# Two feed-forwards whose down projections change orientation: tokens x 512 columns, summed in SBUF and turned by TensorE

## The chip, the cores and the metric

The kernel runs on one core of a Trainium2 chip. The metric is the device time of one execution in microseconds, the median of several runs. One further execution was taken with the hardware profiler; its rows are what the prediction reads. A core has TensorE (PE, with its weight loads shown apart as PEld), VectorE (DVE), ScalarE (ACT), GpSimd (POOL) and SyncE (SP), which here issues the DMAs. Each engine works through its own queue in order, and PE writes only to PSUM, of which there are eight banks of 128 x 512 fp32 words.

## The reference, cut to what matters

A trunk of two layers on 256 tokens of width 2048, all in fp32. Each layer has a mixer and a convolutional feed-forward, with adaptive shift, scale and gate vectors computed from one conditioning vector `c`. This case is about the feed-forwards and the normalisation in front of them:

```python
def conv_ffn(h, w_up, conv_w, conv_b, w_down):
    u = causal_dwconv(h @ w_up, conv_w, conv_b)      # 2048 -> 2 x 5632, three taps over tokens
    a, b = jnp.split(u, 2, axis=-1)
    return (jax.nn.silu(a) * b) @ w_down             # 5632 -> 2048

def reference(...):
    ...
    for i in range(2):
        mod = (c_act @ ada_w[i] + ada_b[i])[:, None, :]
        sh1, sc1, g1, sh2, sc2, g2 = jnp.split(mod, 6, axis=-1)
        h = rms_norm(x, norm_g[i, 0]) * (1.0 + sc1) + sh1
        y = even_mixer(h, ...) if i % 2 == 0 else odd_mixer(h, ...)
        x = x + g1 * y
        h = rms_norm(x, norm_g[i, 1]) * (1.0 + sc2) + sh2
        x = x + g2 * conv_ffn(h, ffn_w_up[i], ffn_conv_w[i], ffn_conv_b[i], ffn_w_down[i])
    return x
```

## The kernel before

The residual `xT` stays in SBUF with channels on the partitions: 16 tiles (`kt`) of 128 channels x 256 tokens. The feed-forward's 5632 hidden channels are 44 blocks of 128, dealt into four quarters of 11 (`QK`); a quarter first computes 22 up blocks (`a` and `b` of each hidden block in turn), then goes down with the 11 gated blocks of that quarter as its k range.

**Numbers.** Most products are made from two fp32r parts. ACT copies a piece of a raw weight to `whi` (L133), and DVE, or POOL, subtracts to get the rest, `wlo` (L139). Activations have the same two parts: `h` (from `Modulated`, L529 to L537) and `g`, the gated product (L678 on ACT, L679 on DVE). A product is hi x hi, hi x lo and lo x hi: three matmuls. Where weights are given whole, as `raw`, one fp32 matmul does it (L360).

**Orientation.** `mm_t` has the weight block as the stationary operand and the 256 tokens as columns; the result is channels x tokens, as `xT` wants it. With `pair`, which the second feed-forward uses, both token parts of the activation are sent as one matmul of 512 columns and the third as 256 (L349 to L353), and two halves of the bank are added afterwards (L689, L690). Without it there are three of 256 (L356 to L358). `mm_n` has 128 tokens as the stationary operand and up to 512 weight columns moving (L367 to L369, for the odd mixer's projections); its result is tokens x channels.

**Order.** The order on each engine is written by the code, with some helpers. `W.take()` gives the next weight piece (at most 1024 columns a partition) and has the split of the piece two further on written first (`AHEAD`); three buffers each of raw, `whi` and `wlo` are there. Every `take()` also runs `advance()`, which writes one step of each open chain in `steps` and starts one from `waiting`; `hook()`, which runs one entry of `hooks`; and `tick()`, which writes an adaptive product `ada` (DVE, L269) when the credit reaches one; `rate["ada"]` is added per piece. `W.share` is the part of the `wlo` subtractions that go to POOL, a quarter in the first feed-forward and none in the second; while `W.hold` is set, none goes to POOL and no `ada` is written. A modulation value that is needed and not there yet is computed on the spot (`modulation`).

**The start of a feed-forward.** The first seven up blocks (`FIRST`; six blocks, `FIRST_U`, in the odd mixer's input projection) are run as `h.outer(n)`: for each `kt`, raw fp32 weights against `xT` scaled by the gain alone, 257 columns, n open banks. While this goes on, the token statistics are finished (at `kt == STATS`, L443), turned into a row on all partitions by two diagonals `SPREAD` steps later (L418, L419, `bc` L454), and the 16 normalised tiles of `h` are made. The early blocks are multiplied by `bc` afterwards into tiles `u` (L709 to L713).

**The end of a quarter.** After the quarter's up blocks one more up block of the next quarter is run; then come 16 down blocks, each summed over 11 k in one bank and added to `xT` times the gate (`add_into_x`, L553). At k = 10 `gated` writes out everything still open (`drain`) and lifts the hold. The last quarter has no further block to run.

## Time and profile before

| | |
|---|---|
| median of 3 runs | 2373.77 us (2373.11 to 2376.73) |
| the profiled execution | 2380.04 us, span from first to last instruction 2378.3 us |
| busy, share of the span | PE 96%, PEld 85%, DVE 75%, ACT 44%, POOL 16% |
| mean granted TensorE clock | 0.988 |
| DMA | 596.36 MB, mean 251 GB/s |

The stages of the profiled execution that matter here are: the even mixer up to 512.98 us; the first feed-forward from there to 1296.25; the odd mixer to 1590.06; the second feed-forward to the end. A window's row gives the length of a stretch, then for each engine its busy time and, in brackets, its instructions, then the granted clock (1.00 is 2.4 GHz), the mean busy share of the DMA engines and GB/s. In a row of a stretch in order of time stand start, duration, engine, line, operation, output <- inputs, shapes and count; the last bracket is idle time ahead of it and what ended that. A raw fp32 matmul shows as two instructions. Matmul durations overlap, so that the pace is read from the starts.

### The profile page before, as it was taken

The page shows a single profiled execution, that of the slowest core. Times are in us where ns is not written, and L with a number is a line of the kernel's source. Part 1 is how long each engine was busy: PE and PEld are TensorE (multiplying, and loading weights), DVE is VectorE, ACT ScalarE, POOL GpSimd, SP SyncE. Part 2 cuts the span into 40 slices and gives each one's busy share as a digit, 9 for nine tenths or more (in the row PEclk, how much of TensorE's full clock was granted, in tenths as well). Part 3 has the DMA queues.
Part 4 walks back from the last instruction along what each step waited for, and adds up shares of the span by engine and source line. Part 5 has one row for each costly group of instructions (what it writes and reads, how often), then busy time and mean ns, then how long its engine had stood idle before and what let it go on. Part 6 is the DMA issues. An engine that isn't in the chain of part 4 may idle for free. (4 is left out here: it accounts for less than half of the span.)

```text
span 2378.3 us, 36086 instructions
## 1 busy us (share of the span) xinstructions
PE 2288.6 (96%) x14056; PEld 2019.1 (85%) x14056; DVE 1786.0 (75%) x2827; ACT 1053.7 (44%) x1884; POOL 379.4 (16%) x238
## 2 busy tenths in 40 slices
PE   6898999999999999999999999999999999999999
PEld 3476677889999999999999777998788888888888
DVE  7758689747968878887986877667976766766765
ACT  2021254116444544544544556447544544554553
POOL 4233435101322222222222020000000000000000
PEclk9999999999999999999999999999999999999999
DMA  9968754776878878978887853556856546545545
GB/s 383 426 231 328 307 197 174 271 264 250 321 264 334 334 283 312 335 281 314 340 301 268 310 203 115 160 171 241 324 182 210 180 157 210 181 156 203 190 150 169
DMA packets 96365, 596.36 MB, mean 251 GB/s; under 512 B 11457, under 2 KB 14145, under 8 KB 44097
## 3 DMA queue, kind: packets, MB, share of 16 engines
q1 hardware_dynamic: 96194, 594.06, 68.4%
q8 instruction: 110, 1.80, 0.3%
q14 instruction: 61, 0.50, 0.1%
HBM read 591.92 MB, written 2.10 MB: 250 GB/s over the span
## 5 line engine op out<-in xcount | busy, mean ns | idle before, releaser
L133 ACT ACTIVATE whi<-raw 128x1024 fp32r<-128x1024 f32 (+2 forms) x659 | 626.8, 952 | 775.3 <-PE bank L357 352.3
L139 DVE TENSOR_TENSOR wlo<-raw,whi 128x1024 fp32r<-128x1024 f32 (+2 forms) x586 | 660.5, 1129 | 366.1 <-ACT whi L133 365.6
L269 DVE CUSTOM_DVE_ANT_0 ada<-ada,cB,adab 128x2048 f32<-128x2048 f32 x192 | 468.9, 2445 | 26.6 <-DMA ada<-adaw 26.0
L352 PE MATMUL bank<-h,whi 128*128 128x512 f32 x1215 | 432.6, 398 | 0.0
L358 PE MATMUL bank<-h,wlo 128*128 128x256 f32 x1328 | 377.3, 284 | 5.5 <-POOL wlo L139 4.9
L356 PE MATMUL bank<-h,whi 128*128 128x256 f32 x1328 | 377.1, 284 | 0.0
L357 PE MATMUL bank<-h,whi 128*128 128x256 f32 x1328 | 376.5, 284 | 0.0
L353 PE MATMUL bank<-h,wlo 128*128 128x256 f32 x1215 | 342.8, 282 | 5.5 <-DVE wlo L139 5.5
L139 POOL TENSOR_TENSOR wlo<-raw,whi 128x1024 fp32r<-128x1024 f32 (+2 forms) x73 | 192.1, 2634 | 667.4 <-ACT whi L133 601.3
L352 PEld LDWEIGHTS bank<-h,whi 128*128 128x128 f32 x1215 | 228.3, 188 | 51.3
L358 PEld LDWEIGHTS bank<-h,wlo 128*128 128x128 f32 x1328 | 255.6, 192 | 6.8 <-POOL wlo L139 5.7
L357 PEld LDWEIGHTS bank<-h,whi 128*128 128x128 f32 x1328 | 255.7, 193 | 0.0
L356 PEld LDWEIGHTS bank<-h,whi 128*128 128x128 f32 x1328 | 255.6, 192 | 0.0
L353 PEld LDWEIGHTS bank<-h,wlo 128*128 128x128 f32 x1215 | 229.4, 189 | 15.2 <-DVE wlo L139 12.0
L352 PE MATMUL bank<-g,whi 128*128 128x512 f32 x640 | 235.2, 407 | 0.9 <-DVE g L679 0.9
L357 PE MATMUL bank<-g,whi 128*128 128x256 f32 x704 | 199.6, 284 | 0.9 <-DVE g L679 0.9
L358 PE MATMUL bank<-g,wlo 128*128 128x256 f32 x704 | 200.1, 284 | 0.3
L356 PE MATMUL bank<-g,whi 128*128 128x256 f32 x704 | 199.3, 283 | 0.8 <-ACT g L678 0.8
L353 PE MATMUL bank<-g,wlo 128*128 128x256 f32 x640 | 182.7, 285 | 0.0
L360 PE MATMUL bank<-hw,raw 128*128 128x256 f32 x640 | 150.7, 390 | 14.1 <-DMA raw<-ev 9.5
L360 PEld LDWEIGHTS bank<-hw,raw 128*128 128x128 f32 x640 | 122.0, 195 | 43.4 <-issue 20.0
L352 PEld LDWEIGHTS bank<-g,whi 128*128 128x128 f32 x640 | 123.7, 193 | 28.7 <-ACT y L697 1.2
(281 smaller groups left out, 3696.9 us busy)
## 6 DMA issues: line engine op xcount, KB each, us to landing
ada<-adaw SPq DMA_DIRECT2D x192, 1024.0 KB, 6.1
raw<-wup SPq DMA_DIRECT2D x162, 1024.0 KB, 5.8
raw<-wdn SPq DMA_DIRECT2D x128, 704.0 KB, 4.2
raw<-out SPq DMA_DIRECT2D x44, 512.0 KB, 3.9
raw<-ev_a SPq DMA_DIRECT2D x16, 1024.0 KB, 4.9
raw<-ev SPq DMA_DIRECT2D x16, 896.0 KB, 14.7
raw<-wup SPq DMA_DIRECT2D x16, 896.0 KB, 4.7
raw<-cmp_w SPq DMA_DIRECT2D x8, 1024.0 KB, 8.5
```

Source lines behind the costliest of these rows:

```text
L133: nc.scalar.activation(hi[:, :n], raw, AF.Copy)
L139: eng.tensor_sub(lo[:, :n], raw, hi[:, :n].bitcast(F32))
L269: V.tensor_tensor_reduce(w, w, cB, 1.0, adab[:, i * 96 + j:i * 96 + j + 1], ALU.mult, ALU.add, m)
L352: PE.matmul(o, hi[:, s_], xx, start=start, stop=False)
L353: PE.matmul(o[:, :T], lo[:, s_], x[:, 0], start=False, stop=False)
L356: PE.matmul(o, hi[:, s_], x[:, 0], start=start, stop=False)
L357: PE.matmul(o, hi[:, s_], x[:, 1], start=False, stop=False)
L358: PE.matmul(o, lo[:, s_], x[:, 0], start=False, stop=stop)
L360: PE.matmul(o, w[:, s_], x, start=start, stop=stop)
```

## The change

In quarters 0 to 2 of both feed-forwards the down projection is done by `down_n`: `mm_n` with the gated block's tokens as the stationary operand and 512 weight columns moving, four chunks of 512 columns, two banks each. ACT copies the first quarter's banks into a tile `acc` (2 x 128 tokens x 2048, fp32, SBUF) and DVE adds those of the next two. During the last quarter's up blocks TensorE transposes `acc` by 128 x 128 blocks (`turn`), and DVE adds the result, times the gate, to `xT`; ten of sixteen `kt` are spread over the up blocks, the last six (`LATE`) stand between the up blocks and the last down projection, which keeps its form. The weights of the three quarters are laid out for this (loads of 4, 4 and 3 k of 512 columns). No up block is moved ahead of a down projection any more. In `gated` the open chains are written out only until the last gate's second part is, and during a hold every `take()` runs `advance()` twice. `FIRST` and `FIRST_U` become five, the statistics are asked for at `kt == 1`, the unsplit `h` moves from ACT to DVE, `u` lies in `acc`, and the rates of `ada` change.

```diff
-FIRST = 7
-FIRST_U = 6
+FIRST = 5
+FIRST_U = 5
+LATE = 6
-STATS = 3
+STATS = 1
-ADA_O = 0.7
+ADA_O = 0.3
-ADA_F0S = 0.4
+ADA_F0S = 0.3
-ADA_F1S = 0.5
+ADA_F1S = 0.1
+ADA_F1U = 0.08
+ADA_F1D = 0.05
...
         w = W.take()
         advance()
+        if W.hold:
+            advance()
         hook()
...
             f = sm.tile([P, T], F32, tag="hf", name="hf")
-            S.activation(f, t, AF.Identity, bias=sh, scale=gs)
+            V.tensor_scalar(f, t, gs, sh, op0=ALU.mult, op1=ALU.add)
...
             def gated(k, q):
                 if k == QK - 1:
-                    drain()
+                    while (q + 1) * QK - 1 not in gates:
+                        advance()
                     W.hold = False
+                    if late:
+                        steps.append(list(late))
+                        late.clear()
                 return gt[q, k // 2][:, k % 2]
+
+            def down_n(q):
+                for c in range(4):
+                    o = [bank() for _ in range(NT)]
+                    k = 0
+                    while k < QK:
+                        w, n = take()
+                        for u in range(n // 512):
+                            mm_n(o, w, slice(u * 512, (u + 1) * 512), gated(k, q), k == 0, k == QK - 1)
+                            k += 1
+                    def add(t, c=c, o=o):
+                        d = acc[:, t, c * 512:(c + 1) * 512]
+                        if q:
+                            V.tensor_tensor(d, d, o[t], op=ALU.add)
+                        else:
+                            S.activation(d, o[t], AF.Copy)
+                    waiting.append([lambda t=t, add=add: add(t) for t in range(NT)])
+
+            def turn(kt):
+                if kt % 2 == 0:
+                    turns[kt // 2] = bank()
+                p = turns[kt // 2][:, kt % 2 * T:(kt % 2 + 1) * T]
+                for t in range(NT):
+                    PE.transpose(p[:, t * P:(t + 1) * P], acc[:, t, kt * P:(kt + 1) * P], ident)
+                g = modulation(i, 80 + kt)
+                return lambda: V.scalar_tensor_tensor(xT[:, kt], p, g, xT[:, kt], op0=ALU.mult, op1=ALU.add)
...
-                for b in range(2 * QK * q + (q > 0) if q else FIRST, min(2 * QK * (q + 1) + 1, 2 * KF)):
+                end = q == NQ - 1
+                if end:
+                    hooks.extend([None] * 6)
+                    for kt in range(KD - LATE):
+                        hooks.append(lambda kt=kt: defer(turn(kt)))
+                        hooks.append(None)
+                for b in range(2 * QK * q if q else FIRST, 2 * QK * (q + 1)):
...
-                    follow(proj_t(h, pair=pair), b // 2, b % 2, ...)
+                    follow(proj_t(h, pair=pair and not last_up), b // 2, b % 2, ...)
                 rate["ada"] = down
-                end = q == NQ - 1
+                if not end:
+                    down_n(q)
+                    continue
+                while hooks:
+                    hook()
+                late.extend(turn(kt) for kt in range(KD - LATE, KD))
                 for kt in range(KD):
```

PE, where the first feed-forward's first quarter turns from up to down; before, with `h` the normalised input and `g` the gated blocks:

```order
L357 MATMUL bank<-h,whi 128x256
L358 MATMUL bank<-h,wlo 128x256
L356 MATMUL bank<-g,whi 128x256
L357 MATMUL bank<-g,whi 128x256
L358 MATMUL bank<-g,wlo 128x256
```

The same place now, where the moving operand is the weight:

```order
L364 MATMUL bank<-h,whi 128x256
L365 MATMUL bank<-h,wlo 128x256
L374 MATMUL bank<-whi,g 128x512
L375 MATMUL bank<-wlo,g 128x512
L376 MATMUL bank<-whi,g 128x512
```

The matmuls of a down quarter become 512 columns wide and half as many.

DVE under the early blocks of the first feed-forward, ahead of the last tiles of `h`, now (`gs` is the gain of a tile, `hf` the unsplit tile, `ada` an adaptive product's weights):

```order
L538 TENSOR_SCALAR hf<-hn,gs,mod 128x256
L544 TENSOR_TENSOR h<-hf,h 128x256
L274 ISA ada,mod<-ada,cB,adab 128x2048
L274 ISA mod 128x1
L274 ISA ada,mod<-ada,cB,adab 128x2048
L274 ISA mod 128x1
L479 SCALAR_TENSOR_TENSOR gs<-mod,normg 128x1
L536 TENSOR_TENSOR hn<-xT,bc 128x256
```

Before, a tile has no `hf` row on DVE, and single products stand between tiles:

```order
L529 TENSOR_TENSOR hn<-xT,bc 128x256
L537 TENSOR_TENSOR h<-hf,h 128x256
L472 SCALAR_TENSOR_TENSOR gs<-mod,normg 128x1
L269 ISA ada,mod<-ada,cB,adab 128x2048
L269 ISA mod 128x1
```

`hf` came to DVE, and two products now stand together ahead of the gain of the last tile.

DVE at the end of the second feed-forward's last up quarter, before (`y<-y` is the last gate product, `g<-y,g` its second part, for which PE waits at k = 10):

```order
L667 SCALAR_TENSOR_TENSOR y<-bank,fcw,y 128x255
L668 SCALAR_TENSOR_TENSOR y<-bank,fcw,y 128x254
L673 TENSOR_TENSOR y<-y 128x256
L679 TENSOR_TENSOR g<-y,g 128x256
L139 TENSOR_TENSOR wlo<-raw,whi 128x640
```

And now:

```order
L676 SCALAR_TENSOR_TENSOR y<-bank,fcw,y 128x255
L677 SCALAR_TENSOR_TENSOR y<-bank,fcw,y 128x254
L682 TENSOR_TENSOR y<-y 128x256
L142 TENSOR_TENSOR wlo<-raw,whi 128x768
L689 TENSOR_TENSOR g<-y,g 128x256
L142 TENSOR_TENSOR wlo<-raw,whi 128x640
```

A weight difference moved in between the gate product and its second part.

## Rows read from the trace of the kernel before

**Rows 1.** Windows by stage: us; PE, PEld, DVE, ACT, POOL busy; clock; DMA; GB/s.
```profile
512.98:562.22 49.24, 49.24 (x233) 43.30 (x232) 24.76 (x69) 24.83 (x61) 2.11 (x1) 1.00 0.67 242
562.22:659.68 97.46, 94.58 (x771) 93.95 (x770) 90.45 (x126) 54.03 (x84) 22.62 (x8) 0.98 0.72 271
659.68:724.10 64.42, 64.06 (x530) 63.51 (x529) 46.44 (x55) 26.89 (x35) 20.86 (x9) 1.00 0.78 283
724.10:851.96 127.86, 126.98 (x1058) 126.78 (x1057) 112.21 (x133) 62.79 (x85) 28.69 (x11) 1.00 0.87 327
...
1296.25:1340.78 44.53, 42.95 (x203) 36.90 (x201) 27.66 (x71) 22.98 (x59) 2.28 (x6) 1.00 0.77 278
1639.30:1738.80 99.50, 94.00 (x515) 77.51 (x513) 95.46 (x148) 60.52 (x102) 0.00 (x0) 1.00 0.76 275
1738.80:1805.15 66.35, 64.05 (x353) 55.19 (x352) 46.21 (x73) 27.95 (x37) 0.00 (x0) 0.97 0.55 190
1805.15:1929.42 124.27, 124.27 (x705) 107.85 (x704) 86.11 (x129) 67.00 (x105) 0.00 (x0) 1.00 0.52 179
2305.39:2378.30 72.91, 65.69 (x353) 56.20 (x351) 43.11 (x70) 26.10 (x36) 0.00 (x0) 0.94 0.50 158
```

**Rows 2.** PE in order of time, odd mixer's second projection; start and duration in us.
```profile
1386.06 0.39 PE L367 MATMUL bank<-whi,h 128*128 128x512 f32 x1
...
1387.42 0.39 PE L367 MATMUL bank<-whi,h 128*128 128x512 f32 x1
```

**Rows 3.** Window of the odd mixer's first such projection, 168 matmuls and four transposes.
```profile
1340.78:1380.97 40.19, 39.34 (x172) 31.58 (x171) 35.42 (x60) 19.42 (x29) 3.89 (x4) 1.00 0.83 317
```

**Rows 4.** PE's waits in the second feed-forward: us in total, times, longest us.
```profile
PE bank L349 <- ACT g L678: 7.1, 4, 2.2
PE bank L353 <- DVE wlo L139: 5.5, 14, 1.0
PE bank L350 <- DVE g L679: 2.0, 3, 0.7
PE bank L352 <- DVE g L679: 0.9, 1, 0.9
```

**Rows 5.** Windows right behind two stops of PE; columns as in rows 1.
```profile
1745.39:1748.80 3.41, 3.41 (x12) 2.82 (x12) 2.20 (x3) 0.74 (x1) 0.00 (x0) 0.50 0.04 17
598.51:601.92 3.41, 3.41 (x18) 3.41 (x17) 3.40 (x2) 0.00 (x0) 1.81 (x1) 0.50 0.93 312
```

**Rows 6.** PE in order of time: eight transposes amid the odd mixer's projections.
```profile
1406.81 1.03 PE L630 MATMUL bank<-ident,n 128*128 128x128 f32 x8
1407.60 0.47 PE L367 MATMUL bank<-whi,h 128*128 128x512 f32 x1
1407.91 0.39 PE L368 MATMUL bank<-wlo,h 128*128 128x512 f32 x1
```

**Rows 7.** DVE in order of time, under the first feed-forward's early blocks (from 512.98).
```profile
514.71 0.43 DVE L433 TENSOR_TENSOR sq<-sq 128x256 f32<-128x256 f32 x1 [0.90 <-ACT sq L429]
...
522.62 0.16 DVE L445 TENSOR_SCALAR rv<-bank 128x2 f32<-128x2 f32 x1 [7.42 <-PE bank L443]
...
525.00 0.48 DVE L418 TENSOR_SCALAR diag<-ident,rsy 128x128 f32<-128x128 f32 x2
...
529.70 0.76 DVE L529 TENSOR_TENSOR hn<-xT,bc 128x256 f32<-128x256 f32 x2
```

**Rows 8.** Groups of DVE by form: count, then busy us, mean ns, idle before.
```profile
L269 DVE CUSTOM_DVE_ANT_0 ada<-ada,cB,adab 128x2048 f32<-128x2048 f32 x192 | 468.9, 2445 | 26.6 <-DMA ada<-adaw 26.0
...
L1487 DVE TENSOR_SCALAR gv<-gv,bmv,rsy 128x1024 f32<-128x1024 f32 x2 | 1.5, 811 | 0.0
```

**Rows 9.** PE's waits in the first feed-forward's first up quarter; columns as in rows 4.
```profile
PE bank L358 <- POOL wlo L139: 2.3, 1, 2.3
```

**Rows 10.** DVE in order of time, first feed-forward's first quarter.
```profile
588.78 2.63 DVE L673 TENSOR_TENSOR y<-y 128x256 f32<-128x256 f32 x1
```

**Rows 11.** POOL in order of time, the same place.
```profile
587.96 3.16 POOL L139 TENSOR_TENSOR wlo<-raw,whi 128x1024 fp32r<-128x1024 f32 x1 [25.49 <-ACT whi L133]
```

More of the change, by code (lines that the diff above doesn't have):

```diff
@@ L199, in want_ffn @@
         for q in range(NQ):
-            for u in range(2 * QK * q + (q > 0), min(2 * QK * (q + 1) + 1, 2 * KF)):
-                if u >= 2 * QK:
-                    W.want(a["wup"][i, u // 2 - QK, u % 2], KD, P)
-            for kt in range(KD):
-                W.want(a["wdn"][i, q, kt], QK, P)
+            for u in range(max(2 * QK * q, 2 * QK), 2 * QK * (q + 1)):
+                W.want(a["wup"][i, u // 2 - QK, u % 2], KD, P)
+            if q < NQ - 1:
+                for c in range(4):
+                    W.want(a["wdn1"][i, q, c], QK, 512)
+            else:
+                for kt in range(KD):
+                    W.want(a["wdn2"][i, kt], QK, P)
     for kt in range(KD):
@@ L660, in ffn @@
             W.share = share
-            half, gt = {}, {}
+            half, gt, gates = {}, {}, set()
+            acc = fp.tile([P, NT, D], F32, name="acc", bufs=1)
+            turns, late = {}, []
             def conv(o, jj, ab):
@@ L705, in ffn @@
             for b in range(FIRST):
-                u = fp.tile([P, T], F32, tag="u", name="u", bufs=FIRST)
+                u = acc[:, 0, b * T:(b + 1) * T]
                 def norm(b=b, u=u):
@@ L720, in ffn @@
                     rate["ada"] = up
-                for b in range(2 * QK * q + (q > 0) if q else FIRST, min(2 * QK * (q + 1) + 1, 2 * KF)):
+                end = q == NQ - 1
[5 more added lines that the diff above has]
+                for b in range(2 * QK * q if q else FIRST, 2 * QK * (q + 1)):
                     if q == 0 and b == FIRST + 4:
                         W.hold = False
-                    if b == 2 * QK * (q + 1) - 1:
+                    last_up = end and b == 2 * QK * (q + 1) - 1
+                    if last_up:
                         W.hold = True
-                    follow(proj_t(h, pair=pair), b // 2, b % 2, *[lambda: None] * (2 if b == FIRST and b % 2 else 0))
+                    follow(proj_t(h, pair=pair and not last_up), b // 2, b % 2, *[lambda: None] * (2 if b == FIRST and b % 2 else 0))
                 rate["ada"] = down
-                end = q == NQ - 1
+                if not end:
[4 more added lines that the diff above has]
+                late.extend(turn(kt) for kt in range(KD - LATE, KD))
                 for kt in range(KD):
-                    if end and kt == KD - 2:
+                    if kt == KD - 2:
                         rate["ada"] = 0.0
-                    if end and kt == KD - 1 and not last:
+                    if kt == KD - 1 and not last:
                         nxt = Modulated(i + 1, 0)
@@ L735, in ffn @@
                     o = proj_t(lambda k: gated(k, q), QK, pair)
-                    then = []
-                    if end:
-                        then = [lambda kt=kt: nc.sync.dma_start(last[:, kt], xT[:, kt])] if last else square_in(kt)
+                    then = [lambda kt=kt: nc.sync.dma_start(last[:, kt], xT[:, kt])] if last else square_in(kt)
                     add_into_x(o, kt, i, 5, then)
@@ L1519, in trunk @@
         rest = out_first(1, mix, 0, [], ready1, 0.0)
-    ffn(1, rest, out, ADA_F1S, 0.0, 0.0, 0.0, True)
+    ffn(1, rest, out, ADA_F1S, ADA_F1U, ADA_F1D, 0.0, True)
 def layout(inputs):
@@ L1569, in layout @@
     a["wup"] = c(wup[:, QK:]).reshape(2, KF - QK, 2, P, D)
-    wdn = np.stack([blocks(w) for w in x["ffn_w_down"]]).reshape(2, KD, P, NQ, QK * P)
-    a["wdn"] = c(wdn.transpose(0, 3, 1, 2, 4))
+    wdn = np.stack([blocks(w[-QK * P:]) for w in x["ffn_w_down"]])
+    a["wdn2"] = c(wdn)
+    wdn = x["ffn_w_down"].reshape(2, NQ, QK, P, 4, 512)[:, :-1]
+    a["wdn1"] = c(wdn.transpose(0, 1, 4, 3, 2, 5)).reshape(2, NQ - 1, 4, P, QK * 512)
     w = x["ev_w_in"][0]
```

8 lines of the change are left out of this document (6 added, 2 removed).

## The prediction

> **What bounds the kernel now.** I read the busy times by stage first, then PE's list of waits, then single stretches in order of time. [rows 1] cut the feed-forwards and the input projection between them into stages; the reader is to set PE's busy time beside the stage's own length. In an up quarter of the first feed-forward PE is busy 126.98 of 127.86 us, in the second 124.27 of 124.27, in a down quarter of the first 64.06 of 64.42. PE sets the pace, and nearly everywhere without a pause; DVE, with 112.21 of 127.86 in the up quarters, comes next, and only where the rows show a wait does it, or POOL, set anything. So an edit is worth what it takes from PE's own instructions or from PE's few waits. These stand at four places: the first quarter of the second feed-forward (99.50 us, DVE busy 95.46), the start of each of its down quarters (66.35 us with PE busy 64.05), its last down quarter (72.91 us, clock 0.94), and one stop in the first feed-forward's first quarter.
>
> Steps from the rows: a block of an up projection costs 127.86 / 22 = 5.81 us in the first feed-forward and 124.27 / 22 = 5.65 in the second (whose wide form sends 512 and 256 columns); an early block, one of the seven in raw fp32, costs 49.24 / 7 = 7.03.
>
> **1. Six of eight down quarters in the other orientation.** Before, a quarter is 16 output blocks x 11 k x 3 matmuls of 256 columns = 528 (in the second, 16 x 11 pairs of 512 and 256). Now it is 4 chunks x 11 k x 2 token halves x 3 = 264 matmuls of 512 columns. The odd mixer's projections have this very form: in an undisturbed stretch it starts every (1387.42 - 1386.06) / 6 = 0.227 us [rows 2], so 264 x 0.2267 = 59.8 us. In the first feed-forward a down matmul takes 64.42 / 528 = 0.1220 against 127.86 / 1056 = 0.1211 in the up quarters, 0.8% more for small waits; with the same share I take 60.3. The other bound is the first such projection as a whole, where DVE has more to do: 40.19 / 168 = 0.239 [rows 3], 63.2 us. I take the clean row, since a down quarter keeps DVE at 46.44 of 64.42 us and that projection kept it at 35.42 of 40.19. First feed-forward: 3 x (64.42 - 60.3) = 12.4 (bounds 3.7 and 13.9).
>
> In the second feed-forward the old quarter also holds a stop: the last gate product comes too late for the eleventh k. The waits of PE give 7.1 us on ACT's copy in four stops, the longest 2.2, so 1.6 in each of the first three, and 0.7 on DVE's second half of it [rows 4]. Behind the stop the clock reads 0.50 for 3.41 us [rows 5], half speed, which loses 1.7: 4.0 us a quarter. In the new form k = 10 comes 10 x 6 x 0.227 = 13.6 us after the quarter's start instead of 10 x 0.35 = 3.5, so the product is there, although it now has one or two weight differences ahead of it on DVE. Its price is in the sum already: 3 x (66.35 - 60.3) = 18.2 (bounds 9.5 and 19.7). The sums in SBUF, 16 copies on ACT and 32 additions on DVE of 128x512, fall where both engines idle and nothing waits for them before the next quarter. Part 1: 30.6 us.
>
> **2. Last down quarters.** They keep their form. In the second the stops are 2.2, 0.9 and 0.2 us [rows 4], and the mean clock of 0.94 over 72.91 loses 4.4, of which I leave 1.4 to the end of the stage, where PE has nothing to do. Twelve transposes now stand ahead (1.2 us), the wide form's joining of two halves is gone for the last block, but the gate's second half waits behind a further weight difference; I leave a stop of 0.6 and no fall of the clock: 3.3 + 3.0 - 0.6 = 5.7 (0 to 7). The first feed-forward's I leave as it is.
>
> **3. Transposes.** 2 x 16 per feed-forward, 64 in all. Eight in a row take 1407.60 - 1406.81 = 0.79 us between two fp32r matmuls [rows 6], 0.099 each: a cost of 6.3. Their additions into x are work for DVE in the last up quarter and replace 3 x 16 of the old ones. The Trainium skill, "TensorE: Matmul & The Clock Gate", Part 4: PE-mode transpose, gives about 275 ns for one in a kernel and says that transposes don't engage the full clock; by that the cost would be 64 x 0.275 = 17.6, an estimate, and the time 11 us longer. The row has a third of it, and the row decides.
>
> **4. Five early blocks for seven (six in the odd mixer).** Four blocks and one move from 7.03 to the pace of the others: 2 x 1.22 + 2 x 1.38 + 1.22 = 6.4 gained. But five blocks take 16 x 5 x 0.44 = 35.2 us instead of 49.24, and under them stand the token statistics and 16 tiles of h. The statistics are now asked for after one k step, 2.2 us in; in the trace the last squares are added 515.14 - 512.98 = 2.2 us in [rows 7]: no margin, some tenths lost each time. From the statistic to the two diagonals DVE needs 525.48 - 522.62 = 2.9 us [rows 7], two k steps last 4.4. Then a tile costs DVE two tensor_tensor of 0.38 (0.76 for two) and, new, the scaling that ACT did: 1024 elements of that form take 0.81 [rows 8], so 256 lie between 0.2 and 0.42, and I take 0.3. Sixteen tiles x 1.06 plus four adaptive products of 2.45 [rows 8] is 26.8 us; from 7.6 it ends at 34.4, just inside 35.2. I set the lost tenths (1.0 for three places) against the 2.3 us by which the odd mixer's 44.53 exceeds 6 x 7.03, of which the lower rate of products should free 1.0: nothing net (bounds +1 and -12, as rival C).
>
> **5. Rates and the hold.** The second feed-forward's first quarter takes 99.50 us for 16 blocks, 9.1 over 16 x 5.65, with PE waiting 5.5 on weight differences [rows 4] and DVE nearly full. Its rate falls from 0.5 to 0.1 products per piece, two pieces a block: 0.8 x 15 x 2.45 = 29 us less on DVE in that stage. What is moved into later quarters meets a DVE with 86.11 of 124.27 us. I leave 1.0: 8.1 gained (6 to 9). The first feed-forward's quarter is 97.46 - 16 x 5.81 = 4.5 over; 2.3 of it is one stop on a POOL difference [rows 9] and 1.7 the half clock behind it [rows 5]. The hold's length is as it was, so I count half: 2.0 (0 to 4).
>
> **Sum:** 30.6 + 5.7 - 6.3 + 6.4 + 8.1 + 2.0 = 46.5 us. It is made in the profiled execution (2380.04 us, span 2378.3), which lies 6.3 above the median of 2373.77; taken from the median it gives **2327.3 us**, 2% faster.
>
> **Rivals.**
> B, the 512-column matmuls run at the 0.239 of the first mixer projection: part 1 gives 13.2 instead of 30.6, 2345 us. For it: weight pieces are now all of 1024 or 512, so the supply is coarser. Against: an up quarter eats the same pieces at 2.9 us each without a stop.
> C, five blocks are too short a cover: DVE ends the tiles late and PE stops at three places for about 2.3 us and then runs at half clock, 4.0 each: 12 us, 2339. For it: the 0.8 us margin, and the two forced products that stand together ahead of the tile before the last.
> F, the gate waits stay, since the differences ahead of the product grow: 3 x 4.0, 2339. Against: 10 us more room.
> T, the clock falls to 1.2 GHz behind the transposes, at 22 places (20 pairs, two runs of twelve): 22 x 1.7 = 37 us, 2364. Against: behind the eight of [rows 6] the next matmul starts 0.31 us after the first, not the 0.43 of half speed. The Trainium skill's "TensorE: Matmul & The Clock Gate", Part 4, would have it so.
> E, slower: the POOL pieces of the first feed-forward. While one runs there, a DVE product of two SBUF tiles of 256, 0.38 us in rows 7, took 2.63 [rows 10], held until POOL's 3.16 us piece ended [rows 11]; such a delay is behind the one stop of rows 9. Pieces in the down quarters grow from 640 and 768 to 1024, and a quarter of 72 goes to POOL: 18. At 2.3 + 1.7 us each, twelve such stops eat the whole gain, and eighteen give 2399. Against: two pieces stand ahead, 5.4 us against 3.2 for a piece, and the old quarters had nine POOL pieces in 64.42 us with 0.4 us of PE idle. The Trainium skill, "SBUF — State Buffer", section SBUF: two separate sides, speaks against longer POOL pieces: it calls the port that DVE and POOL share an exclusive lock for the whole instruction; the two rows agree with it.
>
> **How the numbers follow.** Forecast 0.60 (its own range 2319 to 2337); B 0.15, C 0.10, F 0.05, T 0.03, E 0.07. For eight in ten the range takes the forecast's bounds, F, C and B: 2315 to 2346. About 0.2% (4.7 us) is what a measurement can tell from no change. All cases but E are faster by more; of E I give 0.02 to within 0.2% and 0.05 to slower: faster 0.93, same 0.02, slower 0.05.
>
> **What would show it.** Right: the six down quarters near 60 us at clock 1.00, with no wait on the gate; the second feed-forward's first quarter near 5.7 us a block; 0.1 us a transpose; early blocks near 36 us. Wrong: waits on wlo by POOL in the first feed-forward's down quarters (E), a matmul step near 0.24 (B), waits on hr or on the squares at the early blocks (C). A gain of under 25 us means that part 1 failed.

## The result

The changed kernel takes 2347.47 us (median of 4 runs, 2341.05 to 2349.39) against 2374.27 for the kernel before in the same runs, 27 us faster where 46.5 had been forecast. The ratio of the runs on record is 0.9872, with a 95% interval of 0.9860 to 0.9885; the quotient of the two medians, 0.9887, lies just outside it. The sign was right; the time lies 20 us above the forecast and 1.5 above the range. It is near rival B's 2345, but not by rival B's cause: the new matmuls run at the pace that the forecast gave them.

The two profiled executions differ by 31.4 us of span (2378.3 and 2346.9). The stages of the changed kernel, with the columns of [rows 1]: the first feed-forward's early blocks, first up quarter, first down quarter, second up quarter (without turns) and last up quarter (with turns), then the same five of the second, and its last down quarter.

```profile
512.61:548.93 36.32, 35.78 (x169) 30.96 (x168) 29.73 (x83) 18.29 (x46) 1.11 (x1) 1.00 0.67 238
548.93:651.49 102.56, 99.39 (x818) 98.34 (x817) 84.78 (x119) 55.30 (x83) 23.98 (x9) 1.00 0.75 278
651.49:711.36 59.87, 59.87 (x267) 49.57 (x265) 34.55 (x32) 27.55 (x32) 14.76 (x6) 1.00 0.78 281
711.36:838.07 126.71, 126.71 (x1057) 126.71 (x1056) 110.48 (x133) 64.09 (x88) 31.22 (x11) 1.00 0.89 334
1085.18:1222.11 136.93, 131.29 (x1090) 130.18 (x1088) 117.08 (x146) 63.61 (x88) 29.20 (x11) 1.00 0.84 307
1577.12:1614.04 36.92, 35.91 (x170) 30.97 (x169) 30.53 (x83) 17.41 (x45) 0.00 (x0) 1.00 0.59 209
1614.04:1716.60 102.56, 97.66 (x547) 83.44 (x545) 82.74 (x134) 61.32 (x98) 0.00 (x0) 1.00 0.63 232
1716.60:1777.73 61.13, 60.14 (x265) 49.49 (x264) 34.98 (x37) 28.87 (x36) 0.00 (x0) 1.00 0.64 228
1777.73:1902.10 124.37, 124.37 (x706) 107.89 (x705) 91.02 (x130) 68.51 (x106) 0.00 (x0) 1.00 0.58 210
2148.73:2280.24 131.51, 128.87 (x754) 111.66 (x752) 95.03 (x144) 68.82 (x109) 0.00 (x0) 1.00 0.49 171
2280.24:2346.90 66.66, 62.53 (x355) 53.99 (x353) 43.64 (x72) 23.66 (x31) 0.00 (x0) 0.99 0.52 168
```

An up quarter without turns takes 126.71 to 126.86 in the first feed-forward and 124.37 in the second; a down quarter 59.87 to 60.13 and 61.13. Set against the stages before, with the up blocks that changed quarters counted where they now stand (us gained):

| part | forecast | between the two traces |
|---|---|---|
| six down quarters | 30.6 | 29.0 (13.2 and 15.8) |
| last down quarters | 5.7 | 6.5 |
| turned tiles | -6.3 | -17.3 (10.1 and 7.1) |
| early blocks, rates, up blocks of the first feed-forward | 4.4 | 5.4 |
| the same of the second | 10.9 | 3.5 |
| odd mixer | 1.2, less its lost tenths | 3.9 |

Two rows are wrong: the turns by 11 us and the second feed-forward's start by 7. All rows together miss the 46.5 by 15. The other 5 of the 20 us lie in what the sum was taken from: it was worked out in a profiled execution 6.3 us above its median and then taken off the median, and the changed kernel's profiled execution lies only 1.2 above its own; the traces differ by 31.4, the medians by 26 to 27.

Of PE's waits over the whole span (us in total, times, longest us), those that bear on the change name the turns at once; the waits of [rows 4] on the gate are down to 3.0, in three stops, and one of 0.3 in the last down quarter.

```profile
PE bank L730 <- DVE xT L732: 8.3, 10, 1.6
PE bank L376 <- DVE g L689: 3.0, 3, 1.0
PE bank L360 <- DVE wlo L142: 2.6, 3, 1.1
PE bank L359 <- ACT whi L136: 2.2, 2, 1.4
PE bank L367 <- ACT hr L492: 1.1, 2, 0.5
```

**The turns.** L730 is the transpose, L732 DVE's addition of a turned tile into `xT`. The prediction let a transpose wait for nothing of DVE's. It does wait, since `turn` opens a bank only for even `kt` and writes the odd one into the bank's other half, while DVE still has to read the first half. (Whether the chip or the compiler asks for this wait, no run here shows.) In order of time (PE; then DVE, same place):

```profile
1108.45 0.28 PE L365 MATMUL bank<-h,wlo 128*128 128x256 f32 x1
1110.31 0.44 PE L730 MATMUL bank<-ident,acc 128*128 128x128 f32 x2 [1.58 <-DVE xT L732]
1110.50 0.36 PE L363 MATMUL bank<-h,whi 128*128 128x256 f32 x1
```

```profile
1105.74 2.63 DVE L274 CUSTOM_DVE_ANT_0 ada<-ada,cB,adab 128x2048 f32<-128x2048 f32 x1
1108.31 1.21 DVE L142 TENSOR_TENSOR wlo<-raw,whi 128x1024 fp32r<-128x1024 f32 x1
1109.44 0.41 DVE L689 TENSOR_TENSOR g<-y,g 128x256 fp32r<-128x256 f32 x1
1109.78 0.47 DVE L732 SCALAR_TENSOR_TENSOR xT<-bank,mod,xT 128x256 f32<-128x256 f32 x1
```

The addition has a product, a weight difference and a gate's half ahead of it on DVE, and PE stands until it is done. There are five such stops in each feed-forward, 5.6 us in the first and 2.6 in the second.

**The start of the second feed-forward.** Under the early blocks DVE is busy 30.53 of 36.92 us. The two products that the last tile's gain forces (L274) hold everything behind it. DVE, then ACT, then SyncE's queue:

```profile
1606.49 2.35 DVE L274 CUSTOM_DVE_ANT_0 ada<-ada,cB,adab 128x2048 f32<-128x2048 f32 x1
1608.76 2.34 DVE L274 CUSTOM_DVE_ANT_0 ada<-ada,cB,adab 128x2048 f32<-128x2048 f32 x1
1611.04 0.15 DVE L479 SCALAR_TENSOR_TENSOR gs<-mod,normg 128x1 f32<-128x1 f32 x1
```

```profile
1611.31 0.51 ACT L491 ACTIVATE hr<-xT,gs 128x256 f32<-128x256 f32 x1 [4.64 <-DVE gs L479]
1611.83 1.06 ACT L136 ACTIVATE whi<-raw 128x1024 fp32r<-128x1024 f32 x1
1620.58 1.06 ACT L136 ACTIVATE whi<-raw 128x1024 fp32r<-128x1024 f32 x1 [2.20 <-DMA raw<-wup]
```

```profile
1608.87 2.60 SPq L265 DMA_DIRECT2D ada<-adaw  x2
1611.57 3.18 SPq L123 DMA_DIRECT2D raw<-wup  x2
```

The first split of the up weights starts 2 us before the early blocks end, and the next weight loads stand in SyncE's queue behind two loads that need the products' buffers. Whether that, or what DVE does after it, costs the quarter its 6.5 us (102.56 against 17 blocks of 5.65) was for the runs to tell.

### The profile page after: what moved, and what is told of

It reads as the page before. It is cut to its first block, busy times and chain, and to the rows that moved or that the text cites. A ratio compares the mean times of both kernels' runs of the same rounds, so it can differ in the third digit from the quotient of the medians.

```text
span 2346.9 us, 33916 instructions
## 1 busy us (share of the span) xinstructions
PE 2262.0 (96%) x13128; PEld 1960.7 (84%) x13128; DVE 1766.1 (75%) x2754; ACT 1040.5 (44%) x1811; POOL 375.9 (16%) x232
## 4 chain that ended last, share of the span: by engine, by line
PE 79%; DVE 11%; DMA 5%; ACT 2%; issue 1%; POOL 1%; SPq 0%; ACTq 0%; DVEq 0%; POOLq 0%
PE bank L359 13%; PE bank L365 9%; PE bank L364 9%; PE bank L363 9%; PE bank L367 9%; PE bank L360 7%; PE bank L376 6%; PE bank L375 6%; PE bank L374 6%; DVE ada L274 3%; DMA raw<-ev 2%; PE bank L378 1%; ACT whi L136 1%; DVE cy L1015 1%; DVE ye L1015 1%
## 5 line engine op out<-in xcount | busy, mean ns | idle before, releaser
L136 ACT ACTIVATE whi<-raw 128x1024 fp32r<-128x1024 f32 (+3 forms) x621 | 628.2, 1012 | 806.8 <-PE bank L364 289.0
L142 DVE TENSOR_TENSOR wlo<-raw,whi 128x1024 fp32r<-128x1024 f32 (+3 forms) x554 | 666.0, 1204 | 389.7 <-ACT whi L136 386.5
L274 DVE CUSTOM_DVE_ANT_0 ada<-ada,cB,adab 128x2048 f32<-128x2048 f32 x192 | 465.1, 2427 | 21.8 <-DMA ada<-adaw 21.2
L365 PE MATMUL bank<-h,wlo 128*128 128x256 f32 x1392 | 394.5, 283 | 2.6 <-DVE wlo L142 1.8
L363 PE MATMUL bank<-h,whi 128*128 128x256 f32 x1392 | 395.3, 284 | 0.6 <-ACT whi L136 0.6
L364 PE MATMUL bank<-h,whi 128*128 128x256 f32 x1392 | 393.8, 283 | 0.0
L360 PE MATMUL bank<-h,wlo 128*128 128x256 f32 x1230 | 345.8, 281 | 2.7 <-DVE wlo L142 2.6
L359 PEld LDWEIGHTS bank<-h,whi 128*128 128x128 f32 x1230 | 231.1, 188 | 55.9 <-ACT whi L136 2.9
L363 PEld LDWEIGHTS bank<-h,whi 128*128 128x128 f32 x1392 | 267.1, 192 | 1.0 <-ACT whi L136 0.8
L364 PEld LDWEIGHTS bank<-h,whi 128*128 128x128 f32 x1392 | 267.1, 192 | 0.2
L376 PE MATMUL bank<-whi,g 128*128 128x512 f32 x528 | 205.7, 390 | 3.0 <-DVE g L689 3.0
L375 PE MATMUL bank<-wlo,g 128*128 128x512 f32 x528 | 205.7, 390 | 0.0
L374 PE MATMUL bank<-whi,g 128*128 128x512 f32 x528 | 205.5, 389 | 0.0
L367 PE MATMUL bank<-mixw,raw 128*128 128x256 f32 x512 | 117.4, 392 | 3.3 <-DMA raw<-out 3.2
L376 PEld LDWEIGHTS bank<-whi,g 128*128 128x128 f32 x528 | 99.1, 188 | 24.8 <-DVE g L689 4.2
L378 PE MATMUL bank<-raw,hw 128*128 128x512 f32 (+1 forms) x320 | 117.2, 520 | 1.1 <-DMA raw<-ev_v 1.1
```

The source lines that it names most:

```text
L136: nc.scalar.activation(hi[:, :n], raw, AF.Copy)
L142: eng.tensor_sub(lo[:, :n], raw, hi[:, :n].bitcast(F32))
L274: V.tensor_tensor_reduce(w, w, cB, 1.0, adab[:, i * 96 + j:i * 96 + j + 1], ALU.mult, ALU.add, m)
L359: PE.matmul(o, hi[:, s_], xx, start=start, stop=False)
L360: PE.matmul(o[:, :T], lo[:, s_], x[:, 0], start=False, stop=False)
L363: PE.matmul(o, hi[:, s_], x[:, 0], start=start, stop=False)
```

## The experiments

Each is told by its ratio to the kernel before, run in between on the same chip, and by its stages. A difference between two changed kernels is one of medians from different groups of runs; the kernel before reads 2374.27 to 2376.22 in these, so that one of 2 to 3 us alone says nothing. Those that change the code ahead of a line shift its number by a few.

**A bank for each early turn.**

```
-                if kt % 2 == 0:
+                if kt % 2 == 0 or kt < KD - LATE:
                     turns[kt // 2] = bank()
```

> Each of the ten early turned tiles gets a PSUM bank of its own; in the changed kernel tiles 2n and 2n+1 share one, and there PE waits 8.3 us (10 times) for the vector engine's read of the first half of the bank. Theory (the shared bank is the cost that the prediction missed): these 8.3 us are gone, ff0's last up quarter falls from 136.9 to about 131, ff1's from 131.5 to about 128, the kernel from 2347.5 to about 2339, ratio to the kernel before about 0.9853. Rival (the up quarter with turns costs what it costs since DVE and ACT are late with the split weights while they add tiles into x): the waits move from the bank to the weight halves, and the kernel stays at 2346 to 2348, ratio 0.987.

Measured 2336.94 us (2333.47 to 2339.24), ratio 0.9839 (0.9826 to 0.9851). The two last up quarters:

```profile
1083.69:1213.86 130.17, 130.17 (x1090) 130.07 (x1088) 116.48 (x146) 63.82 (x88) 29.59 (x11) 1.00 0.88 324
2141.42:2268.62 127.20, 127.20 (x753) 111.54 (x752) 94.94 (x144) 68.91 (x109) 0.00 (x0) 1.00 0.51 176
```

PE is busy throughout. 6.8 and 4.3 us are gone, and the kernel is 10.5 faster. What is left over a plain quarter, 130.17 - 126.78 = 3.4 and 127.20 - 124.37 = 2.8, is the 32 transposes at 0.09 to 0.11 each: the prediction's price, without the wait. The waits did not move to the weight halves, as the rival had it.

**Products ahead of the early blocks.**

```
-                    rate["ada"] = ADA_O
+                    rate["ada"] = 0.0 if self.which else ADA_O
-ADA_OUT = 0.45
+ADA_OUT = 0.75
-        rest = out_first(1, mix, 0, [], ready1, 0.0)
+        rest = out_first(1, mix, 0, [], ready1, 0.25)
```

> The modulation products (2.35 us each on DVE) that the changed kernel does under both feed-forwards' early blocks, two by rate and two forced ahead of the last tile's gain, are done earlier, in the output projections of the mixers (about four more in each of these). Theory (first up quarter of ff1 is 6.3 us over its clean step, since the forced pair delays the gain of the last tile, the split of the first weights and, through SyncE's in-order queue, the weight loads behind the products' loads): ff1's first quarter falls from 102.6 to about 98.5, the last tile's wait of 0.54 goes, ff0's first quarter falls by 2 to 3, the output projections stay within 0.5 each, the kernel comes to about 2341, ratio 0.986. Rival (five blocks are a cover of 37 us for work that needs more, whatever the products do): the first quarters stay within 1 us of 102.6 and the kernel at 2346 to 2348. Second rival: the products now hold up the additions into x under the output projections, which become longer by as much as the quarters gain.

Measured 2359.63 us, ratio 0.9929 (0.9914 to 0.9944): 12 us slower than the changed kernel. The first quarters did fall, to 99.64 and 99.09. But the places that took the products pay more: the even mixer ends at 520.8 instead of 512.6, the odd mixer's output projections take 4.6 more, and the second feed-forward's early blocks 5.5 more. PE's waits at the even mixer's end, and then from the odd mixer's output projections to the end of the second feed-forward's early blocks:

```profile
PE bank L367 <- DMA raw<-out: 6.8, 2, 6.1
```

```profile
PE bank L450 <- DVE sq L440: 3.5, 1, 3.5
PE bank L364 <- DVE mix L346: 2.5, 2, 2.0
PE bank L365 <- DVE wlo L142: 2.0, 2, 1.0
```

Where the changed kernel waits 3.2 us for a weight load at the even mixer's end, PE here waits 6.8, with more product loads (1 MB each, on the same queue) about it; and the squares that the statistics need come 3.5 late behind a product, after which the clock is at half for 6.8 us. The second rival held.

**Part four undone: seven and six early blocks.**

```
-FIRST = 5        FIRST_U = 5      STATS = 1       ADA_O = 0.3
+FIRST = 7        FIRST_U = 6      STATS = 3       ADA_O = 0.7
```

> Part four alone undone: seven and six early blocks, statistics after step 3, rate 0.7, as in the kernel before; down projections, turns and the spread of the products later stay. The two traces give five blocks a gain of 2.2 us (ff0) and 3.6 us (ff1), part of the latter from the rates, and 3.9 us for the mixer between. Theory of the prediction (five blocks are worth 6.4 us in the feed-forwards and nothing in the mixer): slower than the changed kernel by about 6, 2354. What the traces say after the result (rates gain nothing while the forced products sit under a shorter cover): slower by about 6 to 10 with the mixer's 3.9 in it, of which 2 to 6 in the feed-forwards. Rival (the five blocks give nothing): 2346 to 2348, with the first quarters of the feed-forwards free of the early waits.

Measured 2354.31 us, ratio 0.9912 (0.9900 to 0.9925): five blocks are worth 6.8, and the prediction's 6.4 was right as a sum, but by luck, since it was not right in its places: early blocks and first quarter together gain 3.0 in the first feed-forward (141.9 to 138.9), 0.6 in the second (140.0 to 139.5), and 3.8 in the odd mixer (293.7 to 289.9), for which the prediction had set its 1.2 against lost tenths.

**Part five alone, in the kernel before.**

```
-ADA_F0S = 0.4    ADA_F1S = 0.5    (up 0.0, down 0.0)
+ADA_F0S = 0.3    ADA_F1S = 0.1    ADA_F1U = 0.08    ADA_F1D = 0.05
```

> The kernel before with only the rates of the gate products changed (0.3 in ff0's first quarter; 0.1, 0.08 and 0.05 in ff1). Prediction's term: 8.1 us in ff1's first quarter (97.46 us to about 89.4) and 2.0 in ff0, so 2364 and ratio 0.9957. Rival (the waits for ACT's gate and the low halves in that quarter come from the start behind the early blocks and not from the products): ff1's first quarter gains under 3 us, 2371 to 2374, ratio 0.999.

Measured 2378.79 us (2371.80 to 2386.43, 12 runs), ratio 1.0015 (1.0006 to 1.0025): no gain, rather a loss. In the profiled run, its fastest, the first quarter of the second feed-forward gains 7.5 (99.50 to 91.96), as forecast, and the down quarter behind it loses 5.5 and the next up quarter 1.1. (The first feed-forward's second up quarter is 1.7 longer too, but it is as long, 129.51, in the last run below, with the old rates.) The products alone, in the first up and first down quarter, of the kernel before (first fence) and of this one (length, DVE's time and count of them, clock, DMA):

```profile
1639.30:1738.80 99.50, 25.77 (x11) 1.00 0.76 275
1738.80:1805.15 66.35, 2.34 (x1) 0.97 0.55 190
```

```profile
1634.78:1726.74 91.96, 7.03 (x3) 1.00 0.60 218
1726.74:1798.56 71.82, 18.76 (x8) 0.98 0.73 258
```

Eight of them are simply done in the down quarter: there every block is added into x times its gate, so all gates are needed in the first down quarter. Only with the sums kept in SBUF is a gate not needed before the turns. Without part one, part five gains nothing.

**hf on ACT again**, in the own-bank kernel.

```
-            V.tensor_scalar(f, t, gs, sh, op0=ALU.mult, op1=ALU.add)
+            S.activation(f, t, AF.Identity, bias=sh, scale=gs)
```

> The own-bank kernel (2336.9) with the full-precision copy of each h tile (hf) scaled by ACT again, as in the kernel before; the change had put it on DVE. Theory (under the three groups of early blocks DVE, busy 14.2 of 15 us there, is the engine that comes late, and hf takes 16 x 0.33 = 5.3 us of it each time): the gain of the last tile and the first weight differences come up to 5 us earlier, the first up quarters fall from 102.3 and 103.5 to about 99, the odd mixer's projections by 1 to 2, the kernel to about 2329, ratio 0.981. Rival (ACT, which then does three scalings a tile, 1.7 us of the 2.2 that a step of five blocks lasts, comes late with hr and with the first weight copies): no gain, or slower with waits on hr, 2336 to 2345.

Measured 2339.21 us, ratio 0.9849 (0.9835 to 0.9862), 2.3 slower than with hf on DVE. The second feed-forward's first quarter fell by 0.7 where 4.5 were expected. The first's rose by 3.5, but there a load reached ACT 4.4 us late (1.4 in the own-bank kernel) and a stretch of 3.41 us at half clock followed, so a loss by hf isn't shown either. The theory that DVE is late because of hf falls.

**One step of deferred work per piece**, in the own-bank kernel.

```
         advance()
-        if W.hold:
-            advance()
```

> The own-bank kernel (2336.9) without the second step of deferred work that the change does for each piece of weights while the hold is on (at the start of the feed-forward's first up quarter and at the start of its last down quarter). Theory (the first up quarters are 4.5 and 6.3 us over their clean step because two steps of normalising and convolving stand ahead of each weight difference on DVE where the kernel before had one): both first quarters fall by 2 to 3, the kernel to about 2332, ratio 0.982. Rival (the excess comes from the late start alone, and the second step only empties the queue earlier): first quarters within 1 us, and the last down quarter of the second feed-forward waits up to 1.5 us for its last gate, 2337 to 2340.

Measured 2330.31 us (2326.32 to 2336.88), ratio 0.9814 (0.9795 to 0.9833), 6.6 faster, though the runs scatter and the interval overlaps the own-bank kernel's; the stages carry the reading. The second feed-forward's first quarter falls from 103.50 to 97.86, 1.8 us over 17 clean blocks. PE's waits in this quarter, with two steps (own bank) and with one:

```profile
PE bank L360 <- DVE wlo L142: 2.6, 3, 1.1
PE bank L359 <- ACT whi L136: 1.6, 2, 0.8
```

```profile
PE bank L358 <- DVE wlo L142: 0.8, 1, 0.8
```

The forced pair ahead of the last tile stands as before; what has gone is the second `advance()`, which put two steps of normalising and convolving ahead of each weight difference on DVE and of each copy on ACT. The quarter holds in every later run with one step: 98.88, 98.09, 98.30 and 99.67, against 102.56, 103.50, 102.85 and 105.90 (old rates) with two. Behind the late start, then, the second step costs 4.0 to 5.6 us (1.7 of the 5.6 is a stretch at half clock in the own-bank kernel's trace). Behind an earlier one this is open: in two runs with two steps the first weight split comes 3.6 to 3.8 us ahead of the quarter instead of 2.2, and the quarter is 3.0 over its clean blocks in one (no products under the early blocks, 99.09) and 6.0 in the other (seven early blocks, 90.81 for 15 blocks; 1.7 of it half clock).

In the first feed-forward it isn't shown: 99.20 here, but 103.62 in a later run ("a faster one" below) of the same instructions there. In that run ACT waited 4.4 us for a load, here 1.5, and behind PE's stop the clock was at half:

```profile
ACT whi L136 <- DMA raw<-wup: 4.4, 1, 4.4
```

```profile
556.04:559.45 3.41, 3.41 (x18) 3.41 (x18) 3.34 (x8) 3.41 (x8) 0.00 (x0) 0.50 0.40 94
```

PE's stops are 2.6 us longer there and the half clock loses 1.7, so these two are the difference of 4.4.

At the last down quarters the single step costs 0.9 and 1.2 us, as the rival said of the second.

**Both of these.** 

> Both: hf on ACT and one step of deferred work per piece, in the own-bank kernel. If both theories hold and their waits are separate: about 2325; if they are the same waits, the better of the two alone, 2329; if both rivals hold, 2337 to 2345.

Measured 2331.96 us, ratio 0.9819 (0.9805 to 0.9834): the one step's gain, and nothing from hf.

**Part five undone**, in the own-bank kernel.

```
-ADA_F1S = 0.1    ADA_F1U = 0.08   ADA_F1D = 0.05
+ADA_F1S = 0.5    ADA_F1U = 0.0    ADA_F1D = 0.0
```

> The own-bank kernel (2336.9) with the rates of the second feed-forward as before (0.5 in the first up quarter, none after it), so part five undone behind the new down projections. Theory of the prediction (29 us of products more on DVE in that quarter cost 8 us there): first quarter from 103.5 to about 111, nothing back in later quarters, 2345, ratio 0.9875. Rival (in the kernel before, the same rates alone saved 7.5 in that quarter and gave it back in the down and up quarters that followed; with products back in the first quarter the later ones are free of them): the quarter costs 8 and the later ones give 1 to 3 back, 2341. Second rival (with five blocks the first quarter is bound by its start alone): within 2 us of 2337.

Measured 2342.80 us, ratio 0.9860 (0.9847 to 0.9874): the rates are worth 5.9, but in other places. The first quarter, with 13 products instead of 3, is only 2.4 longer; the first down quarter takes 1.2 more and the last one 4.2 (70.90 against 66.69). There the turns of the last tiles force two products on DVE just ahead of the last gate:

```profile
2270.57 2.35 DVE L274 CUSTOM_DVE_ANT_0 ada<-ada,cB,adab 128x2048 f32<-128x2048 f32 x1
2272.85 2.35 DVE L274 CUSTOM_DVE_ANT_0 ada<-ada,cB,adab 128x2048 f32<-128x2048 f32 x1
```

```profile
2277.82 0.38 PE L356 MATMUL bank<-g,wlo 128*128 128x256 f32 x1 [2.44 <-ACT g L692]
2278.57 0.80 PE L357 MATMUL bank<-g,whi 128*128 128x512 f32 x1 [0.37 <-DVE g L689]
```

The stop is 2.8 us against 0.3, and 3.41 us at half clock follow, which lose 1.7: that is the 4.2. So the change without its rates gains only 2.0 of the 6.3 us of the last down quarter, because the turns then force products there. The rates alone, in the kernel before, gain 1.1 there (72.91 to 71.85) and leave its old stop. The prediction had counted none of this for the rates.

**A faster one.** One step at the start, two at the start of the last down quarter, and two for the pieces of the first chunk of the second feed-forward's down quarters, with a bank for each early turn:

```
-        if W.hold:
+        for _ in range(extra[0]):
             advance()
...
+                    extra[0] = int(pair and c == 0)
...
+                        extra[0] = 1
```

> The own-bank kernel with one step of deferred work per piece at the start of the first up quarter (2330.3 so far), two at the start of the last down quarter, as in the changed kernel, and two for the pieces of the first 512-column chunk of the second feed-forward's down quarters. Theory (the 1.0 us stop and its trail in each of these down quarters is the last gate's second half, one of some six steps that advance only once per piece of two k, so that it comes at the eleventh k): the three quarters fall from 61.13 to 59.9, the two last down quarters from 66.0 and 67.9 back to 65.1 and 66.7; the kernel to about 2325, ratio 0.979. Rival (the weight differences of the chunk's pieces come late behind the doubled steps): quarters at 61 or above with waits on the differences, 2328 to 2331.

Measured 2323.69 us (2320.65 to 2325.29), ratio 0.9774 (0.9758 to 0.9791), 24 us faster than the changed kernel. The down quarters of the second feed-forward are at 59.85, with no stop:

```profile
1701.41:1761.26 59.85, 59.85 (x265) 49.57 (x264) 34.99 (x37) 28.77 (x36) 0.00 (x0) 1.00 0.67 233
```

**The forced pair by the rate**, in that kernel.

```
-ADA_O = 0.3
+ADA_O = 0.5
```

> The kernel before this one in the list with the rate of products under the early blocks at 0.5 for 0.3, so that the two products forced ahead of the last tile's gain are done earlier by the rate. Theory (the 0.9 us stop on the last tile's hr at both feed-forwards, and the late weight split behind it, come from the forced pair): 1 to 2 us less at each, ratio 0.978. Rival (DVE is full there, so the products only move ahead of other tiles, or the rate lets in more products than the pair): no gain or up to 5 us slower, with other waits on h or on the first differences.

Measured 2337.47 us, ratio 0.9830 (0.9810 to 0.9850), 14 slower, where the rival had said up to 5: the early blocks take 38.98, 39.62 and 40.76 for 36.32, 35.58 and 36.91. The rival's cause held. In each feed-forward the products are the same four (five for three in the odd mixer). The forced pair is gone, but each product now stands ahead of other tiles on a DVE that is busy 23.5 of 24 us there either way, and ACT's scaled tile comes late for PE. PE's waits from the second feed-forward's early blocks into its first quarter:

```profile
PE bank L367 <- ACT hr L492: 1.9, 2, 1.2
PE bank L359 <- ACT whi L136: 1.6, 1, 1.6
```

**Twice the POOL pieces**, in the same kernel (rival E).

```
-LO_F = 0.25
+LO_F = 0.5
```

> The kernel first in this list with POOL's share of the weight differences in the first feed-forward doubled, from 0.25 to 0.5, which doubles what the slower rival of the prediction (E) lives on: a POOL piece of 1024 holds up DVE's work beside it until PE stops for 2.3 us and half clock follows. By that rival: down quarters of the first feed-forward over 65 with waits on the differences, the kernel 20 to 70 us slower. By the forecast (POOL's pieces are asked for two ahead and cost PE nothing as long as 5 us pass between them): down and up quarters within 1 us of 59.9 to 60.2 and 126.8, the kernel within 4 us.

Measured 2349.87 us, ratio 0.9883 (0.9865 to 0.9901), 26 slower. The first feed-forward's second up quarter, at 0.25 and then at 0.5:

```profile
708.53:835.24 126.71, 126.71 (x1057) 126.71 (x1056) 110.45 (x131) 64.09 (x88) 31.20 (x11) 1.00 0.89 335
```

```profile
712.12:846.11 133.99, 127.73 (x1057) 126.92 (x1056) 117.69 (x120) 63.77 (x88) 68.28 (x22) 1.00 0.85 315
```

11 more pieces on POOL, 11 fewer instructions on DVE, and DVE is busy 7 us longer. DVE and POOL in order of time there:

```profile
796.43 3.40 DVE L142 TENSOR_TENSOR wlo<-raw,whi 128x1024 fp32r<-128x1024 f32 x1
...
803.26 1.22 DVE L142 TENSOR_TENSOR wlo<-raw,whi 128x1024 fp32r<-128x1024 f32 x1
804.39 2.63 DVE L682 TENSOR_TENSOR y<-y 128x256 f32<-128x256 f32 x1
```

```profile
795.79 2.96 POOL L142 TENSOR_TENSOR wlo<-raw,whi 128x1024 fp32r<-128x1024 f32 x1 [3.76 <-ACT whi L136]
803.83 2.91 POOL L142 TENSOR_TENSOR wlo<-raw,whi 128x1024 fp32r<-128x1024 f32 x1 [5.09 <-ACT whi L136]
```

A weight difference of DVE's that meets a POOL piece takes 3.40 for 1.22 and ends at 799.8, a microsecond after the piece. PE then stops for 2.2 to 2.9 us: four times in the first feed-forward's up quarters and once in its third down quarter. The Trainium skill, "SBUF — State Buffer", section SBUF: two separate sides, calls the shared port locked for a whole instruction; these rows agree. The mechanism of rival E is real; at the change's share PE shows no wait for it in the down quarters of 512 columns, at twice the share it takes half of that kernel's gain. But the loss stands mostly where rival E had not put it: the up quarters lose 7.3, 5.6 and 4.0 us, the down quarters 0.5, nothing and 4.6. The forecast's reading (within 4 us) was wrong.

**Parts one to three alone**: the own-bank kernel with seven and six early blocks, hf on ACT, one step, and the rates of before.

```
-FIRST = 5        FIRST_U = 5      STATS = 1       ADA_O = 0.3     ADA_F1S = 0.1 ...
+FIRST = 7        FIRST_U = 6      STATS = 3       ADA_O = 0.7     ADA_F1S = 0.5 ...
```

> The kernel before with parts one to three alone: down projections in 512 columns, sums in SBUF, turned tiles (each early one with a bank of its own); seven and six early blocks, hf on ACT, one step of deferred work per piece, and all rates of products as before. Forecast by the measured pieces: part one gives 12.9 in the first feed-forward and 15 in the second; 32 transposes cost 3.3 and 2.8; without the spread rates two forced products stand at the second last down quarter, which so gains 2 of the 6.3; together 24 less, 2351, ratio 0.990. Rival (what the new downs gain in the second feed-forward needs the rates: with 0.5 in the first quarter DVE is late there and the first down quarter keeps its stop, and the last one all of it): 2356 to 2360, ratio 0.9925 to 0.994.

Measured 2351.60 us (2350.73 to 2352.04), ratio 0.9900 (0.9883 to 0.9916): 24.6 us by the new down projections and turns alone, as forecast from the pieces. In the second feed-forward the first down quarter is 1.3 us longer (62.41) than the other two (61.13).

## Why the prediction was off

**Step 1, the down quarters: right.** 29.0 for 30.6. The step is 59.87 / 264 = 0.2268, the clean row of [rows 2], not the 0.239 of [rows 3]; rival B is out. In the second feed-forward the forecast put the last gate in time for k = 10; it still came 1.0 us late, three times, since deferred work advances once per piece and a piece is now two k. A second advance took that away (61.13 to 59.85). Rival F is there at 1.3 a quarter; at its 4.0 it is out.

**Step 2, the last down quarter: right in size, the cause only in part.** The forecast spoke of stops and of the half clock behind them; with the rates undone 4.2 of the 6.3 come back, by two forced products, their stop and a half clock. The forecast had not tied this to part five.

**Step 3, the turns: a wait overlooked.** The price of a transpose was right: 0.09 to 0.11. The step that failed is "Their additions into x are work for DVE in the last up quarter": the transposes wait for these additions, since two tiles share a bank. This is 10.5 us of the 20, shown by giving each a bank. The clock stays at 1.00 in both last up quarters, so rival T is out. The Trainium skill's 275 ns ("TensorE: Matmul & The Clock Gate", Part 4: PE-mode transpose) is near what one row lasts here, 0.27 us, and not what a transpose costs amid fp32r matmuls; its sentence that transposes don't engage the full clock is not borne out for such pairs.

**Step 4, five early blocks: right as a sum, by luck.** 6.8 for 6.4, more than half of it in the odd mixer, for which 1.2 was forecast; the second feed-forward gave 0.6 of its 2.8. Rival C, stops under too short a cover, is there as 0.5 us on `hr` in each feed-forward and 0.5 on the squares in the second; with the rate under the early blocks at 0.5 the kernel loses 14 us, 10.5 of it in the early blocks, so the margin was as thin as the prediction said.

**Step 5, rates and the hold: the failed step.** Parts four and five were to give 10.9 us in the second feed-forward and gave 3.5; beyond part four's 2.8, that is 0.8 for the 8.1. The rates could give it: alone, in the kernel before, they gained 7.5 in the first quarter, though with 18.7 us of products fewer on DVE (11 to 3) and not 29. The start of the quarter lost it again. "The hold's length is as it was", said of the first feed-forward, looked only at how long it lasts, not at what the change does in it: two steps of deferred work for each piece. Behind a start made late by the forced pair, that cost 4.0 to 5.6 us in the second feed-forward, shown by taking the second step away. In the own-bank kernel the rates are worth 5.9 in all, and 4.2 of that lies at the far end of the kernel.

**The sum.** It was taken from the median, though it held stops of a slower execution; this is 5 of the 20 us.

Own banks and one step together give 2330.3, within 3 us of the forecast 2327.3: these two are the main misses, and the rest, such as those 5 us against 2.7 more than forecast in the odd mixer, nearly cancels, which is luck. Not settled: the first feed-forward's first quarter, 99.20 to 105.83 in runs that differ little there. A load that is issued behind the two forced products' loads reaches ACT 1.4 to 4.4 us late, and in some of the traces half clock follows; why the same load comes earlier in one execution than in another is open. A version that frees that queue was not tried.

## What to carry to other kernels

When work for an idle engine is added, ask first what the bound engine will wait for in return: a tile that it shares with the reader, half by half, ties it to the reader's queue, and a second bank took that away here (a reordering was not tried). A bulk of work that is moved has to be followed to its next deadline; the products that left the first quarter came due in the down quarter until the change of orientation took that deadline away. And a loop that empties deferred work faster is good where PE waits for that work and bad where PE waits for what stands behind it.

## What the runs showed of the hardware

A DVE difference of 1024 elements, 1.22 us alone, took 3.40 beside a POOL piece of the same form, and one of 256 elements, 0.42 alone, took 2.63: DVE, relieved of 11 pieces, was busy 7 us longer. Pairs of 128x128 fp32 transposes between fp32r matmuls cost PE about 0.1 us each, at full clock. One weight load, issued 33.85 us into the first feed-forward both in the own-bank kernel and in the fastest one, took 7.2 us to land in one execution and 10.2 in the other, and ACT waited 1.4 and 4.4 us for it. Behind stops of PE the granted clock reads 0.50 for 3.41 us, in [rows 5] as in the first quarter of the fastest kernel.
